# Even layer's input projections as seven products per pair of column blocks, then one phase in which latent and neighbourhood heads take turns unit by unit

## The chip, the cores and the metric

The kernel runs on one core of a Trainium2 chip. The metric is the device time of one execution in microseconds (us). The kernel before was timed three times, 2625.05 to 2626.97 us, with a median of 2626.67 us.

## The reference

One inference step of a two-layer trunk with 640 tokens of width 2048: 512 latent tokens (a grid of 8 rows by 64 columns) and 128 prompt tokens. Every layer is a normalised and modulated mixer with a residual; shift, scale and gate come from `SiLU(cond) @ w_ada`. The even layer comes first and is the one that changes:

```python
h = rmsnorm(x, g_pre) * (1.0 + scale) + shift
# even layer: 4 x 1024 columns for 8 neighbourhood heads, 512 + 256 + 64 + 1024 for 8 latent heads
qa, ka, va, ga, cq, ckv_raw, kpe, gb = _split(h @ w_in, EVEN_SPLITS)
q_mla = (rmsnorm(cq, g_q) @ w_uq).reshape(B, S, MLA_HEADS, MLA_NOPE + MLA_ROPE)
ckv = rmsnorm(ckv_raw, g_kv)
kb, vb = mla_kv(ckv, kpe, w_ukv)
oa = na_latent(qa, ka, va, ctx_k, ctx_v, rpb)      # window of 8 x 16 keys + 128 cached keys, bias rpb
ob = dense_attention(q_mla, [kb_ctx, kb_lat], [vb_ctx, vb_lat], MLA_SCALE)   # 640 keys
y = concatenate([oa * silu(ga), ob * silu(gb)]) @ w_out
x = x + gate * rmsnorm(y, g_post)
```

(Cut and joined from the reference's functions.) Prompt tokens attend to prompt tokens only. The odd layer has one input projection to q, k, v and g, 2048 columns each, and differential attention in 8 heads.

## The kernel before, in words

**Numbers.** Weights and activations are split into a high and a low part: `w_split` (L92) has ScalarE (ACT) cast a 128x1024 tile to `whi` (L82) and VectorE (DVE) subtract for `wlo` (L83). A product takes three passes on TensorE (PE), high by high, high by low and low by high (`passes`, L223). The 640 tokens stand as groups of 384 and 256 columns (`GROUPS`).

**Stages.** In the start stage (L311 to L380) the input is normalised, transposed and modulated, 256 of its 2048 features at a time, and the columns for `cq`, `ckv` and `kpe` are accumulated in seven tiles `cf`. Beside this run the adaptive-scale products `ada` (L175): bursts of eight tiles `araw` of 128x1024 (0.5 MB each, three buffers) loaded on SP's queue. The even mixer follows:

- the *latent preface*: `latent_norm` (L420) squares `cf` on ACT, sums on DVE, reduces over partitions by the matmuls of L429, takes a root on DVE and POOL, broadcasts by L439 and scales (L442), twice; then `w_uq` (matmuls L482) makes the heads' queries, which go to `qm_dram`;
- eight *latent heads* (L495 to L576): keys and values from `w_ukv` (L541), then for each of four 128-row units scores (L558), row maximum on DVE (L273), exponential with row sum on ACT (L274), normalisation on DVE (L564), five transposes, a cast on ACT and a residual on DVE into `pth` and `ptl`, and the value products (L571). Between heads stands `mla_gate`, the gate's projection;
- eight *neighbourhood heads* (L579 to L663): the same with masks added (L641), a window of two or three key tiles and the cached one, and with the head's q, k, g (and, per two heads, v) projections around it.

**Projections.** `proj_T` (L236, matmuls L233) makes one 128-column block for all tokens, 48 matmuls of 384 and 48 of 256 columns; `proj_nat256` (L252, matmuls L249) makes V of two heads in 240 matmuls of 256 columns. Gates pass a tanh on ACT (L267) and a multiply on DVE (L268). `side_step` puts matmuls of `ada` between.

```python
    def proj_T(srcs, emit, groups=(0, 1)):
        ws = [w_split(s) for s in srcs]
        for g in groups:
            n0, n = GROUPS[g]
            emit(proj_group(ws, g, bank("pj")), slice(n0, n0 + n))
        side_step(SIDE)
```

**The odd layer's form.** The output projection `out_proj` (L672) is followed by the odd layer's projections in another form: two 128-column blocks with the input halved give a 2x2 by 2x2 product, made as seven products instead of eight (`PRODUCTS`, `product` with matmuls L830, 24 each of 320 columns). Seven weight tiles and the input halves' sums (`project_pairs`, L848) are made for it on DVE; the results are added up by DVE and ACT from the PSUM banks (`products`, L896). One product of 28 of the pairs needs only the input and is made ahead, in `out_proj` (`early_products`, L836, `NE`). The odd attention (L1037 to L1201) runs in units of scores, transposes, combination and values, which `step` (L1174) advances by one unit at a time.

**Order.** The order on each engine follows from the program's order and from when buffers come free. Nearly all DMAs are on SP's queue and are issued in order.

## Time and profile before

| | us |
|---|---|
| median of three runs | 2626.67 |
| lowest, highest | 2625.05, 2626.97 |
| the profiled execution, its own time | 2620.83 |
| its span in the trace | 2619.1 |
| PE busy in the span | 2532.0 |
| DVE busy | 1534.5 |
| ACT busy | 1116.3 |
| mean granted clock of TensorE (1 is full) | 0.987 |

The sum of a forecast is made against the profiled execution's own time. Busy time is the time in which an engine had an instruction running; listed durations of single matmuls overlap, since they are pipelined, so a pace is a stretch of time divided by the matmuls in it. A row of busy time by windows reads: the window in us from the span's start, its length, then for PE, PEld (TensorE's weight load), DVE, ACT and POOL the busy time and the number of instructions, the share of full clock that TensorE was granted, the share of DMA engines busy, and GB/s. A row of groups reads: line, engine, operation, output and input names, shapes and types, xcount, busy us, mean ns of one, and the engine's idle time just before with what ended it. A row of a timeline reads: start, duration, engine or queue, line, operation; SPq is SP's issuing of DMAs.

### The profile page before, as it was taken

The numbers are of one execution on the slowest core, as the hardware profiler recorded it, in microseconds if no ns is written. First come the engines' busy times: TensorE is split into PE (matmuls) and PEld (weight loads), VectorE is DVE, ScalarE is ACT, GpSimd is POOL, SyncE is SP. The second block draws the span as 40 slices with busy tenths as digits, with TensorE's granted clock in tenths as the row PEclk, the third lists the DMA queues.
The fourth block names the chain that finished last, engine by engine and source line by source line (L and its number), as shares of the span: only waits on it lengthen the run. The fifth ranks groups of instructions, "written<-read, shape, count | busy, mean of one in ns | idle before, by whom it ended". The sixth has DMA issues, their size and how long they took to land. (4 is left out here: it accounts for less than half of the span.)

```text
span 2619.1 us, 42512 instructions
## 1 busy us (share of the span) xinstructions
PE 2532.0 (97%) x16898; PEld 2299.3 (88%) x16898; DVE 1534.5 (59%) x2492; ACT 1116.3 (43%) x2020; POOL 54.0 (2%) x83
## 2 busy tenths in 40 slices
PE   7999999999999999999899999999999989998997
PEld 5779999899989899988789999999999988777876
DVE  5665654534233333443767677777777757874454
ACT  6333333423223222433555344444444447773333
POOL 0000000000000000000000000000000010000000
PEclk9999999999999999999999999999999999998998
DMA  7773322334444443464887344444444457845465
GB/s 292 267 251 117 128 94 103 117 102 140 132 156 158 137 142 133 163 210 140 262 271 266 129 155 160 157 158 151 151 152 150 141 181 273 300 163 189 161 214 196
DMA packets 217111, 455.78 MB, mean 174 GB/s; under 512 B 59664, under 2 KB 104976, under 8 KB 215248
## 3 DMA queue, kind: packets, MB, share of 16 engines
q1 hardware_dynamic: 209648, 436.80, 49.7%
q0 software_dynamic: 3232, 11.67, 1.3%
q10 hardware_dynamic: 4032, 4.59, 0.5%
q8 instruction: 133, 2.18, 0.3%
q14 instruction: 66, 0.54, 0.1%
HBM read 385.54 MB, written 67.44 MB: 173 GB/s over the span
## 5 line engine op out<-in xcount | busy, mean ns | idle before, releaser
L83 DVE TENSOR_TENSOR wlo<-raw,whi 128x1024 fp32r<-128x1024 f32 x458 | 558.2, 1220 | 504.7 <-ACT whi L82 500.5
L82 ACT CAST whi<-raw 128x1024 fp32r<-128x1024 f32 x458 | 479.1, 1046 | 735.7 <-PE pj L724 156.5
L830 PE MATMUL b<-BT,whi 128*128 128x320 f32 x1600 | 355.0, 311 | 4.3 <-ACT whi L82 4.3
L830 PEld LDWEIGHTS b<-BT,whi 128*128 128x128 f32 x1600 | 269.2, 189 | 4.5 <-ACT whi L82 4.5
L830 PE MATMUL b<-BT,wlo 128*128 128x320 f32 x800 | 248.6, 311 | 0.4 <-DVE wlo L83 0.4
L233 PE MATMUL pj<-act0h,whi 128*128 128x384 f32 x512 | 177.9, 348 | 0.0
L233 PE MATMUL pj<-act0h,wlo 128*128 128x384 f32 x512 | 175.1, 342 | 0.0
L233 PE MATMUL pj<-act0l,whi 128*128 128x384 f32 x512 | 173.6, 339 | 0.0
L830 PEld LDWEIGHTS b<-BT,wlo 128*128 128x128 f32 x800 | 151.1, 189 | 0.8 <-DVE wlo L83 0.8
L233 PE MATMUL pj<-act1l,whi 128*128 128x256 f32 x512 | 146.1, 285 | 0.0
L233 PE MATMUL pj<-act1h,whi 128*128 128x256 f32 x512 | 146.0, 285 | 0.0
L233 PE MATMUL pj<-act1h,wlo 128*128 128x256 f32 x512 | 145.6, 284 | 0.0
L184 PE MATMUL ada<-araw,c_s 128*32 128x256 f32 x1536 | 124.5, 389 | 6.5 <-DMA araw<-in_wada 4.1
L830 PE MATMUL b<-B,whi 128*128 128x320 f32 x512 | 113.1, 309 | 0.0
L233 PEld LDWEIGHTS pj<-act0h,whi 128*128 128x128 f32 x512 | 96.8, 189 | 6.6 <-issue 4.1
L830 PE MATMUL pj<-BT,whi 128*128 128x320 f32 x448 | 99.0, 309 | 0.0
L233 PEld LDWEIGHTS pj<-act0l,whi 128*128 128x128 f32 x512 | 96.7, 189 | 2.1 <-issue 1.6
L233 PEld LDWEIGHTS pj<-act1h,wlo 128*128 128x128 f32 x512 | 98.0, 191 | 0.4
L233 PEld LDWEIGHTS pj<-act1l,whi 128*128 128x128 f32 x512 | 98.1, 192 | 0.1
L233 PEld LDWEIGHTS pj<-act1h,whi 128*128 128x128 f32 x512 | 98.0, 191 | 0.1
L233 PEld LDWEIGHTS pj<-act0h,wlo 128*128 128x128 f32 x512 | 96.6, 189 | 1.2 <-issue 1.2
L273 DVE TENSOR_REDUCE smm<-sc 128x1 f32<-128x640 f32 x80 | 65.4, 818 | 43.3 <-PE sc L558 27.0
(491 smaller groups left out, 6309.7 us busy)
## 6 DMA issues: line engine op xcount, KB each, us to landing
araw<-in_wada SPq DMA_DIRECT2D x192, 512.0 KB, 4.5
raw<-in_wout SPq DMA_DIRECT2D x128, 512.0 KB, 4.3
raw<-in_wEna SPq DMA_DIRECT2D x48, 512.0 KB, 3.3
raw<-in_wOq SPq DMA_DIRECT2D x46, 512.0 KB, 4.0
raw<-in_wOk SPq DMA_DIRECT2D x46, 512.0 KB, 3.8
raw<-in_wOg SPq DMA_DIRECT2D x32, 512.0 KB, 3.9
raw<-in_wOv SPq DMA_DIRECT2D x32, 512.0 KB, 3.8
raw<-in_wE SPq DMA_DIRECT2D x16, 512.0 KB, 3.6
```

What stands on the lines that cost most here:

```text
L82: nc.scalar.copy(out=hi, in_=src)
L83: nc.vector.tensor_tensor(out=lo, in0=src, in1=hi.bitcast(F32), op=sub)
L184: mm(ps[32 * kk:32 * kk + 32, x * 256:(x + 1) * 256], lhsT=c_s[:, 4 * q + kk, :], rhs=raw[:, kk * 256:(kk + 1) * 256], start=(q == 0), sto ...
L233: mm(ps[:, :n], lhsT=w[:, c], rhs=a[:, k], start=(k == 0 and x == 0), stop=(k == KT - 1 and x == 2))
L273: nc.vector.tensor_reduce(out=m, in_=src, op=ALU.max, axis=AX.XY if shape3 else AX.X, negate=True)
L830: mm(out, lhsT=w[:, k * 128:(k + 1) * 128], rhs=b[:, k], start=(opens and k == 0 and y == 0), stop=(k == KH - 1 and y == 2), skip_group_ch ...
```

## The change

The even layer's projections take the odd layer's form. `PAIRS` lists for layer 0 four pairs of gate blocks of the latent heads ("m") and, for each neighbourhood head, k with v and q with g: 20 pairs of seven products. `early_products`, `project_pairs` and `products` get the layer as a parameter; `NE` is (20, 28), so every pair of layer 0 has one product made early. The token groups become 320 and 320, and in the start stage `ht`, the modulated input, is also stored to `h_dram`, from where the halves are read back on POOL's queue to make the sums. The seven `cf` tiles are stored to `cf_dram` and read back after the products. All projected blocks go to `pj_dram` (gates with their tanh done, `plain_steps` and `store1`), and each head loads its own.

Behind the products a new PSUM pool is opened (`sc` twice, `tr` and `po` once), the preface runs with `side_step` between its blocks, and then one loop over eight head indices: `start_mla` and `start_na` make the operands of a latent and a neighbourhood head (V of the latter is now transposed on PE), and their units (four and a prompt unit each) alternate in `even_step`: the scores of this unit, the transposes of the last, the values of the one before it, with one or two `ada` steps in turn. The normalisation of a unit moves from DVE to ACT (`normalised`). The output projection takes its weights and heads in the order in which they end (`KORDER0`). The odd layer's work is as before. Core of the diff:

```diff
-GROUPS = ((0, 384), (384, 256))
+GROUPS = ((0, NH), (NH, NH))
-NE, NE1 = 28, 12
+NE = (20, 28)
+NE1 = (4, 8)
...
+    h_dram = [dp.tile([KT, 128, 2, NH], F32, name=f"h_dram{l}") for l in range(2)]
+    cf_dram = [dp.tile([128, NT], F32, name=f"cf_dram{b}") for b in range(7)]
...
+            nc.sync.dma_start(out=h_dram[0][ks].rearrange("k p h n -> p k (h n)"), in_=ht)
...
+        for b in range(7):
+            for x, sl in zip(halves(cf[b]), (slice(0, NL), slice(NL, NT))):
+                nc.sync.dma_start(out=cf_dram[b][:, sl].rearrange("p (h n) -> p h n", h=2), in_=x)
...
+    PAIRS = ([("m", b, "m", b + 1, (i["wE"][b], i["wE"][b + 1])) for b in range(0, 8, 2)]
+             + [(r0, hd, r1, hd, (i["wEna"][hd, x0], i["wEna"][hd, x1])) for hd in range(NA_HEADS)
+                for r0, x0, r1, x1 in (("k", 1, "v", 3), ("q", 0, "g", 2))],
+             [(r0, b, r1, b, (i[w0][b], i[w1][b])) for b in range(2 * DIFF_HEADS)
+              for r0, r1, w0, w1 in (("k", "g", "wOk", "wOg"), ("q", "v", "wOq", "wOv"))])
...
+    def early_products(l, act0):
+        for g in range(NE[l]):
+            out = bank("pj")[:, :NH]
+            product(out, w_split(PAIRS[l][g][4][0][1]), [x[:, KH:] for x in act0], True)
+            xs = xp.tile([128, NH], F32, tag="xs1", bufs=2, name="xs1")
+            nc.scalar.copy(out=xs, in_=out)
+            nc.scalar.dma_start(out=p2_dram[l][g], in_=xs)
+            yield
...
+            def plain_steps(xs, kind, b):
+                if kind == "m":
+                    th = sp.tile([128, 2, NH], F32, tag="th", name="th")
+                    nc.scalar.activation(out=th, in_=xs, func=AF.Tanh, scale=0.5)
+                    nc.vector.scalar_tensor_tensor(out=xs, in0=th, scalar=1.0, in1=xs, op0=ALU.add, op1=ALU.mult)
+                for x, sl in ((xs[:, :, :HL], slice(0, NL)), (xs[:, :, HL:], slice(NL, NT))):
+                    nc.sync.dma_start(out=pj_dram[0][kind][b][:, sl].rearrange("p (h n) -> p h n", h=2), in_=x)
+                if kind == "k":
+                    nc.sync.dma_start(out=o["na_kT"][b].rearrange("p (h n) -> p h n", h=2), in_=xs[:, :, HL:])
+                yield
...
+    xp = space(even, "xs")
+    project_pairs(0, act0, spare, early_products(0, act0))
+    even.close()
+    banks_.close()
...
+    pp = space(banks_, "ps1", True)
+    twice[:] = ["sc"]
...
+    side = (x for l, c in [(0, (16 + n, 17 + n)) for n in range(0, 8, 2)] + [(1, (n, 8 + n)) for n in range(8)]
+            for x in ada(l, c))
...
+    for b in range(7):
+        nc.sync.dma_start(out=cf[b], in_=cf_dram[b])
...
+        for name, src, n in (("kc", i["na_kcT"][hd], 128), ("qf", pj_dram[0]["q"][hd], NT), ("kf", pj_dram[0]["k"][hd], NT),
+                             ("vf", pj_dram[0]["v"][hd], NT), ("vc", i["na_vc"][:, hd * 128:(hd + 1) * 128], 128),
+                             ("sg", pj_dram[0]["g"][hd], NT)):
+            x[name] = np_.tile([128, n], F32, tag=name, bufs=2, name=name)
+            nc.sync.dma_start(out=x[name], in_=src)
+        return x
...
+    def normalised(e, z):
+        nc.vector.reciprocal(out=z, in_=z)
+        nc.scalar.activation(out=e, in_=e, func=AF.Copy, scale=z)
...
+            def scores():
+                ps = half2(bank("sc"))
...
+                        mm(ps[:, h, :NH], lhsT=q, rhs=k[:, h * NH:(h + 1) * NH], start=(n == 0), stop=(n == 4))
+                s["e"] = e = m2.tile([128, NT], F32, tag="e", bufs=3, name="e")
+                z = m2.tile([128, 1], F32, tag="z", bufs=4, name="z")
+                softmax(m2, ps[:, :, :NH], half2(e), z, True)
+                normalised(e, z)
+            def turned():
+                if t % 2 == 0:
+                    H["p"] = [m2.tile([128, 5, 256], F32R, tag=f"pt{n}", name=f"pt{n}") for n in "hl"]
+                pt = bank("tr")
+                transpose_to(pt, s["e"], 5)
+                c = slice((t % 2) * 128, (t % 2 + 1) * 128)
+                hi_lo(pt[:, :NT].rearrange("p (t c) -> p t c", t=5), *[y[:, :, c] for y in H["p"]])
+            def values():
+                if t % 2 == 0:
+                    return
+                if t == 1:
+                    H["po"] = bank("po")
+                po = H["po"]
+                for b in range(5):
+                    for n, (v, pr) in enumerate(passes(vh, vl, *H["p"])):
+                        mm(po[:, (t - 1) * 128:(t + 1) * 128], lhsT=v[:, b, vs], rhs=pr[:, b],
+                           start=(b == 0 and n == 0), stop=(b == 4 and n == 2))
+                if t == 3:
+                    gated(po, x["sg"], slice(0, NL))
+            return scores, turned, values
+        kpf_ = kpf[rows]
...
+    def even_step(u=None):
+        if u is not None:
+            u[0]()
+        if late:
+            late[0][1]()
+        if ends:
+            ends.pop(0)[2]()
+        if late:
+            ends.append(late.pop(0))
+        if u is not None:
+            late.append(u)
+    loads = [(load_mla(0), load_na(0))]
+    n_unit = 0
+    for hd in range(8):
+        xm, xn = loads.pop()
+        for t, units in enumerate(zip(start_mla(hd, xm), start_na(hd, xn))):
+            if t == 1 and hd < 7:
+                loads.append((load_mla(hd + 1), load_na(hd + 1)))
+            for u in units:
+                even_step(u)
+                side_step(1 + n_unit % 2)
+                n_unit += 1
+    even_step()
```

PE at the end of the first norm: `po` and `tr` are the norm's PSUM tiles, `pj` that of a projection, `act0` the input, `BT` an input sum of the seven products, `araw` a tile of `w_ada`. Before:

```order
L233 MATMUL pj<-act0h,whi 128x384
L233 MATMUL pj<-act0l,whi 128x384
L429 MATMUL po<-ones,acc 128x8 x5
L439 MATMUL tr<-dg,ones 128x128 x2
L233 MATMUL pj<-act0h,wlo 128x384
L233 MATMUL pj<-act0h,whi 128x384
L233 MATMUL pj<-act0l,whi 128x384
L439 MATMUL tr<-dg,ones 128x128 x2
```

and with the change:

```order
L352 MATMUL pj<-BT_2244,whi 128x320 x2
L352 MATMUL pj<-BT_2244,wlo 128x320
L191 MATMUL ada<-araw,c_s 32x256 x28
L624 MATMUL po<-ones,acc 128x8 x5
L191 MATMUL ada<-araw,c_s 32x256 x4
L179 MATMUL ada<-ident,ad 128x128 x3
L624 MATMUL po<-ones,acc 128x8 x5
L179 MATMUL ada<-ident,ad 128x128
L634 MATMUL tr<-dg,ones 128x128 x5
L676 MATMUL sc<-cqh,whi 128x384
```

The norm's matmuls stood between matmuls of a gate's projection; now they stand behind the last product, between `ada` steps, and `w_uq` (L676) follows at once.

The norm's operands `cf` are loaded on SP behind the last stores of the products and two more `araw` tiles (seven loads of L583, 128x640 each); before, they were still in SBUF.

SP in the first stage (`araw` tiles of `w_ada`, `wS` the weights of `cf`). Before:

```order
L182 DMA araw<-in_wada 128x1024 x8
L89 DMA raw<-in_wS 128x1024
L89 DMA raw<-in_wS 128x768
L399 DMA gsub<-in_diff_g 128x2
L182 DMA araw<-in_wada 128x1024 x8
```

and with the change:

```order
L189 DMA araw<-in_wada 128x1024
L314 DMA h_dram_138<-ht 128x2x640
L189 DMA araw<-in_wada 128x1024 x7
L95 DMA raw<-in_wS 128x768
L95 DMA raw<-in_wS 128x1024
```

The store of `ht` (L314) is new and stands behind the first tile of a burst, ahead of the other seven.

ACT within two heads (`e` the exponentials, `smm` the row maximum, `z` the row sum, `pth` the cast transposes). Before, in a latent head:

```order
L274 ACTIVATE e,z<-sc,smm 128x640
L82 CAST qh<-raw 128x512
L82 CAST qph<-raw 128x512
L274 ACTIVATE e,z<-tr,smm 128x640
L82 CAST pth<-sc 128x5x128
L82 CAST pth<-tr 128x5x128
L274 ACTIVATE ep,zp<-tr,smm 128x128
L267 ACTIVATE sg<-pj 128x384
L307 COPY ep<-tr 128x128
L82 CAST whi<-raw 128x1024 x2
```

and with the change:

```order
L245 ACTIVATE e,z<-sc,smm 128x640
L88 CAST pth<-tr 128x2x128
L731 ACTIVATE e<-e,z 128x640
L88 CAST pth<-tr 128x128
L876 COPY e<-sc 128x128
L245 ACTIVATE e,z<-e,smm 128x512
L88 CAST pth<-tr 128x5x128
L731 ACTIVATE e<-e,z 128x512
```

The casts of weights and the gates' tanh are gone from here, the normalisation (L731) is new, and a latent unit (640 wide) and a neighbourhood unit (512 or 384) follow each other.

## Rows read from the trace of the kernel before

**Rows 1.** Windows: busy time in the start stage and the even mixer, and the sum.
```profile
0.00:196.30 196.30, 176.07 (x1389) 135.29 (x1390) 117.87 (x280) 84.94 (x153) 3.48 (x12) 1.00 0.77 270
196.30:1098.00 901.70, 894.36 (x6611) 826.06 (x6610) 395.31 (x739) 298.65 (x612) 2.85 (x2) 1.00 0.38 127
...
sum 2619.00, PE 2532.01 PEld 2299.31 DVE 1534.53 ACT 1116.26 POOL 53.97; mean PE 506.40 PEld 459.86 DVE 306.91 ACT 223.25 POOL 10.79
```

**Rows 2.** Windows: matmuls of L249, L233, L830 alone (PE and PEld only).
```profile
842.90:871.80 28.90, 28.90 (x240) 28.80 (x240) 1.00 0.41 137
...
901.20:915.30 14.10, 14.10 (x96) 14.04 (x96) 1.00 0.53 188
...
1339.00:2147.00 808.00, 795.54 (x5376) 792.19 (x5376) 0.99 0.50 165
```

**Rows 3.** Windows: the latent preface, all engines, then L482 alone (PE, PEld).
```profile
196.30:265.00 68.70, 67.38 (x446) 65.11 (x445) 41.21 (x71) 27.02 (x46) 2.85 (x2) 0.98 0.34 119
...
217.70:262.50 44.80, 44.26 (x288) 42.00 (x288) 1.00 0.44 153
```

**Rows 4.** Timeline: the first norm’s matmul and the first cast behind it.
```profile
200.50 1.28 PE L429 MATMUL po<-ones,acc 128*128 128x8 f32 x10
...
211.53 0.73 ACT L82 CAST cqh<-cf 128x640 fp32r<-128x640 f32 x1 [8.97 <-DVE cf L442]
```

**Rows 5.** Groups on ACT: the even mixer; last row: the odd attention.
```profile
L82 ACT CAST whi<-raw 128x1024 fp32r<-128x1024 f32 x91 | 95.4, 1048 | 183.3 <-PE pj L233 98.8 <-PE pj L249 68.4 <-PE pj L541 7.7
L274 ACT ACTIVATE e<-sc,smm 128x640 f32<-128x640 f32 x16 | 12.7, 796 | 44.9 <-DVE smm L273 44.9
...
L82 ACT CAST pth<-tr 128x640 fp32r<-128x640 f32 x16 | 11.1, 696 | 6.9 <-PE tr L172 6.7
...
L267 ACT ACTIVATE sg<-pj 128x384 f32<-128x384 f32 x16 | 7.9, 492 | 10.9 <-PE pj L233 8.9 <-DMA raw<-in_wE 1.3 <-DMA raw<-in_wEna 0.7
...
L267 ACT ACTIVATE sg<-pj 128x256 f32<-128x256 f32 x15 | 5.7, 377 | 0.0
...
L1133 ACT ACTIVATE e<-e,z 128x640 f32<-128x640 f32 x32 | 26.7, 835 | 2.1 <-DVE z L1131 1.8
```

**Rows 6.** Groups on DVE: the even mixer.
```profile
L83 DVE TENSOR_TENSOR wlo<-raw,whi 128x1024 fp32r<-128x1024 f32 x90 | 110.3, 1225 | 204.8 <-ACT whi L82 204.5
L564 DVE TENSOR_SCALAR e<-e,z 128x640 f32<-128x640 f32 x32 | 17.7, 552 | 0.8
...
L273 DVE TENSOR_REDUCE smm<-sc 128x1 f32<-128x640 f32 x16 | 13.2, 824 | 27.0 <-PE sc L558 27.0
...
L83 DVE TENSOR_TENSOR ptl<-tr,pth 128x640 fp32r<-128x640 f32 x16 | 13.2, 824 | 5.1 <-ACT pth L82 5.1
...
L268 DVE SCALAR_TENSOR_TENSOR sg<-sg,pj 128x384 f32<-128x384 f32 x16 | 8.9, 554 | 5.0 <-ACT sg L267 4.9
...
L645 DVE TENSOR_SCALAR e<-e,z 128x512 f32<-128x512 f32 x16 | 7.7, 482 | 0.3
L645 DVE TENSOR_SCALAR e<-e,z 128x384 f32<-128x384 f32 x16 | 6.7, 420 | 0.5
...
L268 DVE SCALAR_TENSOR_TENSOR sg<-sg,pj 128x256 f32<-128x256 f32 x15 | 6.2, 414 | 0.0
```

**Rows 7.** Windows: odd attention, first 24 us, steady part, last 16 us.
```profile
2150.00:2174.00 24.00, 15.70 (x72) 14.67 (x71) 10.03 (x19) 8.90 (x19) 2.51 (x5) 0.67 0.96 345
...
2198.00:2354.00 156.00, 151.91 (x1185) 126.23 (x1184) 128.06 (x315) 118.67 (x309) 12.80 (x15) 1.00 0.71 247
2354.00:2370.00 16.00, 10.58 (x65) 8.74 (x64) 11.31 (x20) 10.88 (x29) 0.00 (x0) 0.89 0.50 158
```

**Rows 8.** Timeline of SP, first stage: two bursts of ada tiles.
```profile
66.00 12.30 SPq L182 DMA_DIRECT2D araw<-in_wada  x8
...
83.54 12.74 SPq L182 DMA_DIRECT2D araw<-in_wada  x8
```

More of the change, by code (lines that the diff above doesn't have):

```diff
@@ L30 @@
 LAM_INIT = 0.8 - 0.6 * math.exp(-0.3 * 1)
+KORDER0 = [b for p in range(4) for b in (8 + 2 * p, 9 + 2 * p, 2 * p, 2 * p + 1)]
 NA_SCALE = 128 ** -0.5
@@ new lines, in model @@
+        nc.sync.dma_start(out=gpost, in_=i["gpost"])
+        accs = cycle("pj", "sc", "po", "pj")
+        for p in range(8):
+            if p == 0:
+                run(first)
+            ws = [w_split(i["wS"][p, :, 0:1024]), w_split(i["wS"][p, :, 1024:1792], 768)]
+            ht = cfp.tile([128, 2, NT], F32, tag="ht", bufs=2, name="ht")
+            for kk in range(2):
+                k = 2 * p + kk
+                for g, (n0, n) in enumerate(GROUPS):
+                    for m, sl in ((0, slice(0, HL)), (1, slice(HL, NH))):
@@ L495, in model @@
[L495 to L503 removed]
+            ks = slice(2 * p, 2 * p + 2)
+            for g, (n0, n) in enumerate(GROUPS):
+                hi_lo(ht[:, :, n0:n0 + n], act[g][0][:, ks], act[g][1][:, ks])
@@ new lines, in model @@
+            nc.sync.dma_start(out=h_dram[0][ks].rearrange("k p h n -> p k (h n)"), in_=ht)
+            if p < 7:
+                run(ada(0, (p + 1, 9 + p), "tr"))
+            for b in range(7):
+                hi, lo = ws[b // 4]
+                for g, (n0, n) in enumerate(GROUPS):
+                    ps = next(accs)
+                    for kk in range(2):
+                        c = ((b % 4) * 2 + kk) * 128
+                        for x, (w, a) in enumerate(passes(hi, lo, *act[g])):
+                            mm(ps[:, :n], lhsT=w[:, c:c + 128], rhs=a[:, 2 * p + kk],
+                               start=(kk == 0 and x == 0), stop=(kk == 1 and x == 2))
+                    dst = cf[b][:, n0:n0 + n]
+                    if p == 0:
+                        nc.scalar.copy(out=dst, in_=ps[:, :n])
+                    else:
+                        nc.vector.tensor_tensor(out=dst, in0=dst, in1=ps[:, :n], op=ALU.add)
@@ new lines, in product @@
+    def product(out, ws, bt, opens):
+        for k in range(KH):
+            for y, (w, b) in enumerate(passes(*ws, *bt)):
+                mm(out, lhsT=w[:, k * 128:(k + 1) * 128], rhs=b[:, k], start=(opens and k == 0 and y == 0),
+                   stop=(k == KH - 1 and y == 2), skip_group_check=True)
+    p2_dram = [[dp.tile([128, NH], F32, name=f"p2_{l}_{g}") for g in range(NE[l])] for l in range(2)]
+    def early_products(l, act0):
[6 more added lines that the diff above has]
+            yield
@@ new lines, in start_mla @@
+        ps = half2(bank("sc"))
+        for h in range(2):
+            for b in range(2):
+                w0 = (e2 * 2 + b) * 128
+                for n, (w, a) in enumerate(passes(hi[:, w0:w0 + 128], lo[:, w0:w0 + 128], ckh, ckl)):
+                    mm(ps[:, h, :384], lhsT=w, rhs=a[:, b, h * 384:(h + 1) * 384], start=(b == 0 and n == 0),
+                       stop=(b == 1 and n == 2))
+        hi_lo(ps[:, :, :384], half2(kh), half2(kl))
+        nc.scalar.copy(out=kf, in_=ps[:, 1, 256:384])
@@ L658, in model @@
-                nc.scalar.copy(out=osb[:, :NL], in_=po)
-                nc.scalar.copy(out=osb[:, NL:], in_=prompt_T_out(np_, [(qf[:, NL:], kf)], vp[:, vs]))
-                sg = np_.tile([128, NT], F32, tag="sg", bufs=2, name="sg")
-                proj_T(i["wEna"][hd, 2], lambda ps, sl: silu2(ps, sg[:, sl]))
-                gate_store(((osb, slice(0, NT)),), sg, 0, hd)
-        run(side)
+                gated(po, sg, slice(0, NL))
+            return scores, turned, values
+        return [unit(b) for b in range(4)] + [prompt_unit(np_, [(qf[:, NL:], kf[:, NL:])], vp, sg, hd)]
@@ new lines, in model @@
+    late, ends = [], []
+    def even_step(u=None):
[20 more added lines that the diff above has]
+                n_unit += 1
```

1031 lines of the change are left out of this document (464 added, 567 removed).

## The prediction

> **What bounds the kernel now.** First read the busy time by stage. In the whole span TensorE (PE) is busy 2532 of 2619 us, and in the even layer's mixer, from 196.3 to 1098.0 us, 894.4 of 901.7; VectorE (DVE) and ScalarE (ACT) are busy 395 and 299 us there [rows 1]. The change lives in that stage, so the question is what PE has to do in it and what else could come to hold it up. I cut the 901.7 us into three parts.
>
> *Projections.* Counts over clean stretches give the true pace of matmuls, without the overlap that their listed durations contain [rows 2]: one 128-column block by `proj_T` (48 matmuls of 384 columns, 48 of 256) takes 14.1 us, a 256-column pair by `proj_nat256` (240 matmuls of 256 columns) 28.9 us. The mixer has 32 of the first and 4 of the second: 451 + 116 = 567 us.
>
> *Latent preface.* From 196.3 to 262.5 us there are the norms and the `w_uq` products, plus one gate projection of 14.1 us: 66.2 - 14.1 = 52 us, of which the `w_uq` matmuls take 44.8 [rows 3].
>
> *The rest.* 902 - 567 - 52 = 283 us, or 35.4 us per head pair (one latent and one neighbourhood head): attention and the adaptive-scale matmuls (`ada`), with the projections interleaved as cover for every softmax wait.
>
> **The change part by part.**
>
> *Seven products instead of eight.* The odd layer runs this form already: 5376 matmuls of 320 columns in 808 us, so 0.1503 us each, all its waits included [rows 2]. The even layer gets 20 pairs of 7 x 24 = 168 matmuls, 3360 in all: 505 us. Against 567 that is **-62 us**. Its weight sums are four DVE operations per pair as in the odd layer, without the rope that the odd layer adds, and the odd layer keeps its pace with DVE as loaded as that. The making of the five operands lies beside the 20 early products, about 71 us of PE work. I put it at nothing more. Bounds: at 0.147 us, the pace inside one projection block (14.1/96), 494 us; with 10 us for operands that come late, 515.
>
> *A preface without cover.* Now the gate projection hides the norm chain. After the change the PSUM pool changes hands, the seven `cf` tiles come back from DRAM, and the order of PE has seven `ada` steps and then the norm's matmuls. SP issues the `cf` loads behind the last stores of the products. From the first norm matmul at 200.50 us to the end of a first cast at 212.26 us the chain took 11.8 us [rows 4]. The loads ahead of it, 2.3 MB of `cf` and three 0.5 MB `ada` tiles, take 14 us at the 270 GB/s of the first stage [rows 1]. Together about 25 us, then the 45 us of `w_uq`: 70 instead of 52, **+18**. Bounds of the gap: 12 us if the loads are hidden, 40 if the second norm and the loads line up behind the first.
>
> *Attention alone.* This is the term that decides. ACT in the stage before is 298.65 us; the change takes 80 of the 91 weight casts away from here (80 x 1.048 = 84) and the tanh (13.6), the preface has about 25 of its own [rows 3, 5], and it adds the normalisation, which moves from DVE: 32 latent units at 0.835 us, the odd layer's price for the same, and 32 smaller ones for which I take 0.6, in proportion to columns (46 us). So ACT comes to 222 us. DVE: 395.3 - 80 x 1.225 (98) - 15 (gates) - 32 (normalisation) - 39 (preface) = 211 [rows 3, 6]. PE, an estimate from the paces of [rows 2] (0.147 us for 320 columns, 0.12 for 256, and 0.12 for what is narrower too): 40 score matmuls of 320 columns, 12 of 384 for keys, 75 of about 256, 39 transposes and some 60 narrow `ada` matmuls per head pair, about 28 us, 222 in all. Three engines, then, each with 26 to 28 us per head pair, and no projection between them. That they overlap fully gives 28 us; no stage does.
>
> The nearest row is the odd layer's attention, which runs the same kind of loop: in its steady part 156 us for six heads, 26.0 each, with DVE busy 21.3 and ACT 19.8 [rows 7]. By DVE, 26.4 x 26.0/21.3 = 32; by ACT, 27.8 x 26.0/19.8 = 36.5. I take 34, and 16 us for filling and draining, as the odd loop's last stretch has it [rows 7]: 8 x 34 + 16 = 288 us. Against 283 that is **+5**, with 3 us for the first head's queries, which make a round trip through DRAM: **+8**. Ends: 238 us (28 per head) and 366 us (the serial chain, below).
>
> *Start.* The activations are also stored to `h_dram`, 5.2 MB, from the queue that loads the `ada` tiles. That is 19 us at 270 GB/s if nothing hides it, nothing if all is hidden. SP issues eight tiles in 12.3 us and the next burst starts at 83.54, so some 5 of 17.5 us are nearly free [rows 8]; but the store stands behind the first tile of a burst and must wait for `ht`, and the other seven are queued behind it. I take **+6**. Groups of 320 and 320 columns cost what 384 and 256 did; the extra small ACT and DVE operations (four for three) lie beside PE, at worst 4 us.
>
> *Handover to the output projection.* The last head's gate projection used to cover it: **+2**, above the drain counted already. All later stages are the same work.
>
> Sum: -62 + 18 + 8 + 6 + 2 = -28 us. The profiled execution took 2620.8 us (span 2619.1 and 1.7 around it), so 2593 by its own clock; it lies 5.8 us below the median of the timed runs, 2626.67, and on that scale the forecast is **2599 us**.
>
> **A rule against it.** In the odd attention's first 24 us PE was busy for 15.7 and its granted clock was 0.67, a mix of the two levels; in the 156 us that followed PE was busy 97% and the clock 1.00 [rows 7]. The Trainium skill, "TensorE: Matmul & The Clock Gate", "Why this matters for your kernels", says that idle gaps between bursts of matmuls put the array back to half its clock. The first of these rows agrees with it, the second shows a loop of this kind that escapes. For the sum I use the second. Were the loop to run at 0.67 throughout, its 27.8 us of PE work would take 41.5 per head, 348 us in all instead of 288.
>
> **The rivals.**
>
> *The units run one after another (slower).* `tr` has one buffer, so a unit's transposes wait until the previous unit's residual has left it, and each softmax passes DVE, ACT, DVE, ACT. Laid end to end, a latent unit costs max 0.824, exponential 0.796, normalisation 0.835, cast 0.696 and residual 0.824 [rows 5, 6], with sums and reciprocals about 4.3 us; the neighbourhood unit about the same with its mask added and two casts. A pair of units is 8.7 us, four pairs and about 9 us for the head's own splits and prompt units 43.7 us: 366 us, 2677. If half the overlap is lost, 39.5 us per head, 332 us and **2643 us**. It decides from 38 us per head on. For it: three engines equally loaded, a chain that crosses between two of them, and no filler but `ada`. Against it: the order on ACT puts another unit's cast or exponential into nearly every wait, and the odd loop reaches 82% of DVE.
>
> *The loop comes near its engines' bound (faster still).* At 30 us per head 256 us, **2567 us**. For it: two independent streams, and 15 `ada` steps to fill PE. Against it: the odd loop does not.
>
> *The clock falls in the loop*, as priced above: **2659 us**.
>
> *The saving is given back by the edges.* A gap of 40 us, 19 in the start, 10 in the operands: 2599 + 15 + 13 + 10 = **2637 us**. That the change does not do what it says would show here too: 3360 matmuls at a pace of 0.165 would save 13 us instead of 62. The same loop in the odd layer speaks against that.
>
> **How the numbers follow.** A measurement of this kernel tells 0.2%, 5 us, from no change. The forecast, 32 to 36.5 us per head with edges as taken, spans 2580 to 2622 and gets 0.56; nearly all of it is faster. The fast rival gets 0.14, the serial one 0.20, the clock 0.03, the edges 0.07. Faster: 0.54 + 0.14 + 0.01 = 0.69. Within 0.2% (2621 to 2632): 0.02 of the forecast, 0.05 of the serial case where it is mildest and 0.03 of the edges, 0.10. Slower: 0.21. The range goes down to 2562, past the fast rival's 2567, and up to 2648, past 2643 and 2637; what lies outside is a loop at its bound below, the fully serial chain and the low clock above, about 0.2. The forecast's own range is 2580 to 2622.
>
> **What would show it.** Right: the products of the even layer at 0.150 us per matmul and 505 us; a PE gap of some 25 us behind them; a head pair every 34 us, with ACT and DVE each busy about 80% of it and PE's clock near 1.00; the first stage ending near 203 us instead of 196. Wrong: a head pair over 38 us with PE waiting for normalised rows and ACT for row maxima means the serial rival; a clock below 0.9 in the loop the clock; `wlo` or `tf` as PE's releaser in the products a DVE that the sums overload; and SP sitting at the `h_dram` store while `ada` waits for its tiles a start that is dearer than 6 us.

## The result, and the profile after

The changed kernel is slower by 0.7%: 2644.9 us, median of four runs (2639.08 to 2647.45), against 2626.04 for the kernel before; the ratio is 1.0069, with a 95% interval of 1.0050 to 1.0087. The forecast was 2599 with 69% for faster; the range, up to 2648, held the time, but the sign was wrong. In what follows a ratio compares with the kernel before as timed in the same session, and a total without a ratio is a single execution, of which it can't be told whether it was a slow one.

The busy time by stage of the changed kernel, cut at its own stage bounds (start, products, the gap to the first `w_uq` matmul, `w_uq`, the loop over head pairs, all that follows), columns as in [rows 1]:

```profile
0.00:208.70 208.70, 180.07 (x1377) 137.19 (x1378) 120.36 (x291) 87.39 (x166) 6.10 (x16) 0.98 0.78 276
208.70:704.00 495.30, 493.52 (x3366) 492.80 (x3368) 340.04 (x369) 208.26 (x291) 3.57 (x5) 1.00 0.48 159
704.00:742.60 38.60, 15.41 (x98) 8.87 (x97) 13.10 (x33) 7.45 (x12) 2.88 (x2) 0.58 0.85 288
742.60:792.40 49.80, 49.77 (x315) 46.37 (x315) 29.76 (x51) 21.46 (x40) 0.00 (x0) 0.95 0.48 148
792.40:1122.40 330.00, 297.28 (x2225) 226.09 (x2221) 204.06 (x481) 203.74 (x476) 0.00 (x0) 0.96 0.64 214
1122.40:2640.90 1518.50, 1460.03 (x8897) 1337.28 (x8897) 1020.85 (x1471) 731.77 (x1253) 47.53 (x69) 0.98 0.57 190
```

Against the stages of before, with the forecast of each term:

| stage | before, us | after, us | difference | forecast |
|---|---|---|---|---|
| start | 196.3 | 208.7 | +12.4 | +6 |
| projections / products | 567 | 495.3 | -71.7 | -62 |
| preface (gap and `w_uq`) | 52 | 88.4 | +36.4 | +18 |
| attention with `ada` | 283 | 330.0 | +47.0 | +8 |
| the rest | 1521.1 | 1518.5 | -2.6 | +2 |

The differences sum to 21.5, that of the two spans is 21.8 (2640.9 - 2619.1). So the products gave more than was forecast, and the start, the preface and the loop took it back. In the loop PE is busy 297 of 330 us, and DVE and ACT 204 each: what the forecast had as three equal engines is one engine well ahead of two.

In the gap, what PE waited for (the waits of PE, 704.0 to 742.6 us; total, times, longest):

```profile
PE ada L191 <- DMA araw<-in_wada: 16.9, 4, 7.9
PE po L624 <- DVE acc L622: 2.9, 2, 2.1
```

And SP's queue at the same time, as a timeline:

```profile
708.68 0.42 SPq L523 DMA_DIRECT2D pj_g<-xs  x1
709.20 0.88 SPq L189 DMA_DIRECT2D araw<-in_wada  x2
710.13 3.73 SPq L583 DMA_DIRECT2D cf<-cf_dram  x7
715.45 0.33 SPq L599 DMA_DIRECT2D lamb<-in_lam  x1
```

The products' last store (L523) is issued at 708.68; only then come the `ada` tiles and `cf`. PE's first norm matmul stands behind `ada` matmuls that wait for these tiles, and they make up the longest wait. They are not what held the norm, though. Its matmuls began when their operand `acc` was ready, 2.09 us after the last of these `ada` matmuls; DVE, ACT and PE in time order:

```profile
721.43 0.23 DVE L658 COPY kpf<-cf 128x128 f32<-128x128 f32 x1 [13.16 <-DMA cf<-cf_dram]
723.08 0.20 ACT L604 ACTIVATE lam<-lam 128x2 f32<-128x2 f32 x1 [15.33 <-DVE lam L603]
723.19 0.72 ACT L618 ACTIVATE acc<-cf 128x640 f32<-128x640 f32 x1
725.53 1.08 PE L191 MATMUL ada<-araw,c_s 128*32 128x256 f32 x8 [1.11 <-DMA araw<-in_wada]
728.71 2.30 PE L624 MATMUL po<-ones,acc 128*128 128x8 f32 x10 [2.09 <-DVE acc L622]
```

The squares that make `acc` (L618 and behind) could start only at 723.19: a copy of a `cf` tile on DVE waited for its load until 721.43, a small exponential for the odd layer (`lam`) stood behind that copy and behind its own load, issued at 715.45 behind `cf`, and the first square stood behind the exponential on ACT. So the late loads held the norm, by way of DVE and ACT.

The steady part of the loop, from the keys of the second head to those of the eighth (six head pairs): first everything, then the `ada` matmuls of L191 alone (PE and PEld), and below them PE's longest waits in it:

```profile
840.60:1076.10 235.50, 222.10 (x1705) 169.08 (x1705) 148.02 (x362) 152.50 (x360) 0.00 (x0) 0.99 0.71 235
...
840.60:1076.10 235.50, 54.34 (x552) 15.06 (x552) 0.99 0.71 235
```

```profile
PE ada L191 <- DMA araw<-in_wada: 5.0, 7, 1.3
PE tr L179 <- DVE ptl L89: 4.1, 6, 1.0
```

A head pair takes 39.25 us, PE is busy for 37.0 of it: 9.1 in the `ada` matmuls and 28.0 in the rest, nearly all of it attention. DVE has 24.7 and ACT 25.4. The loop's 330 us are eight times 39.25 and 16 for filling and draining.

### The profile page after: what moved, and what is told of

The parts are those of the page before. It is cut to its first block, busy times and chain, and to the rows that moved or that the text cites. A ratio compares the mean times of both kernels' runs of the same rounds, so it can differ in the third digit from the quotient of the medians.

```text
span 2640.9 us, 42310 instructions
## 1 busy us (share of the span) xinstructions
PE 2496.1 (95%) x16266; PEld 2248.6 (85%) x16266; DVE 1728.2 (65%) x2695; ACT 1260.1 (48%) x2237; POOL 60.1 (2%) x91
## 5 line engine op out<-in xcount | busy, mean ns | idle before, releaser
L88 ACT CAST whi<-raw 128x1024 fp32r<-128x1024 f32 (+1 forms) x518 | 542.2, 1047 | 853.2 <-PE pj L995 161.5
L89 DVE TENSOR_TENSOR wlo<-raw,whi 128x1024 fp32r<-128x1024 f32 (+1 forms) x518 | 631.3, 1220 | 443.7 <-ACT whi L88 439.1
L352 PE MATMUL b<-BT,whi 128*128 128x320 f32 x2560 | 567.1, 310 | 4.3 <-ACT whi L88 4.3
L352 PEld LDWEIGHTS b<-BT,whi 128*128 128x128 f32 x2560 | 429.9, 189 | 4.5 <-ACT whi L88 4.5
L352 PE MATMUL b<-BT,wlo 128*128 128x320 f32 x1280 | 396.7, 310 | 0.4 <-DVE wlo L89 0.4
L191 PE MATMUL ada<-araw,c_s 128*32 128x256 f32 x1536 | 147.4, 405 | 35.6 <-DMA araw<-in_wada 35.2
L352 PEld LDWEIGHTS b<-B,whi 128*128 128x128 f32 x832 | 139.1, 188 | 0.0
L352 PE MATMUL pj<-act0h,whi 128*128 128x320 f32 x416 | 130.1, 313 | 6.8 <-ACT xs L363 6.8
L352 PE MATMUL pj<-act0h,wlo 128*128 128x320 f32 x416 | 129.4, 312 | 0.0
L352 PE MATMUL pj<-act0l,whi 128*128 128x320 f32 x416 | 129.4, 311 | 0.0
L352 PE MATMUL b<-act0h,whi 128*128 128x320 f32 x416 | 128.5, 309 | 0.0
L191 PEld LDWEIGHTS ada<-araw,c_s 128*32 128x32 f32 x1536 | 40.1, 110 | 83.2 <-DMA araw<-in_wada 47.8
L245 ACT ACTIVATE e<-sc,smm 128x640 f32<-128x640 f32 x96 | 76.6, 798 | 28.6 <-DVE smm L244 27.1
```

What stands on the lines that cost most here:

```text
L88: nc.scalar.copy(out=hi, in_=src)
L89: nc.vector.tensor_tensor(out=lo, in0=src, in1=hi.bitcast(F32), op=sub)
L191: mm(ps[32 * kk:32 * kk + 32, x * 256:(x + 1) * 256], lhsT=c_s[:, 4 * q + kk, :], rhs=raw[:, kk * 256:(kk + 1) * 256], start=(q == 0), sto ...
L245: nc.scalar.activation(out=dst, in_=src, func=AF.Exp, bias=m, accum_out=z)
L352: mm(out, lhsT=w[:, k * 128:(k + 1) * 128], rhs=b[:, k], start=(opens and k == 0 and y == 0), stop=(k == KH - 1 and y == 2), skip_group_ch ...
```

## Experiments

**What sets the loop's pace.** Theory A: PE's own work. Theory S, the serial rival of the prediction: the chain of a unit (maximum, exponential, normalisation, cast, residual). The first run takes all `ada` work out of the loop, and out of the preface.

```diff
-    make_cond()
     side = (x for l, c in ...
...
-                side_step()
     pre_.close()
...
                 even_step(u)
-                side_step(1 + n_unit % 2)
...
     even_step()
+    mctx.close()
+    mctx = ExitStack()
+    mp_ = space(mctx, "mod2")
+    make_cond()
     run(side)
     mctx.close()
```

> All ada steps of the preface and the loop run behind the loop, one after another, with no cover; the loop then holds attention alone. Theory A (the loop stands at PE's own work, some 34 us per head pair of which ada is 8 to 9): the loop, 330 us from its first w_ukv matmul to its last values in the changed kernel, takes 260 to 280 us. Rival S (the softmax chain of the units sets the pace, and ada only fills its waits): it takes 315 us or more. The total is longer in both, since 96 tiles of 0.5 MB have then to be loaded alone, about 170 us.

The loop took 290.1 us (total 2783.49): neither's number. The six steady head pairs (816.5 to 1017.4 us), and PE's longest waits in them:

```profile
816.50:1017.40 200.90, 168.49 (x1114) 151.15 (x1113) 143.73 (x321) 146.16 (x348) 0.00 (x0) 0.97 0.35 103
```

```profile
PE tr L179 <- DVE ptl L89: 11.0, 8, 1.8
PE sc L806 <- ACT e L245: 6.0, 10, 1.4
```

33.5 us per head pair, with PE busy 28.1, DVE 24.0, ACT 24.4. So attention by itself does take longer than any engine's work, and what PE waits for is the units' chain: residuals (`tr` for `ptl`, 11.0 us of that stretch) and exponentials (`sc` for `e`, 6.0). But `ada` is no filler in these waits: 9.1 us of it per head pair lengthen the pair by 5.8.

The second PSUM buffer of the scores goes to the transposes instead, on top of the version whose `ada` tiles come behind the preface (its diff stands with the gap, below):

```diff
-    twice[:] = ["sc"]
+    twice[:] = ["tr"]
```

> As the run without ada in the preface, but in the loop tr has two PSUM buffers and sc one. If the single tr holds the units up (a unit's transposes wait for the residual of the one before, the serial rival's reason), the loop falls from 332 to 315 or less; if the scores need the second buffer more, it rises to 345 or more; within 8 us, neither sets the pace.

The loop rose from 332.4 to 356.5 us (total 2658.71): the scores need the second buffer more than the transposes do. What `tr` would gain from one of its own, beside the two of the scores, this run can't show. The changed loop's waits bound it: PE waits there for residuals in `tr` for 4.1 of 235.5 us, 0.7 per head pair, so the serial rival's reason plays little part with `ada` in the loop.

```diff
-        nc.scalar.activation(out=e, in_=e, func=AF.Copy, scale=z)
+        nc.vector.tensor_scalar(out=e, in0=e, scalar1=z, scalar2=None, op0=ALU.mult)
```

> The units' normalisation goes back to DVE (0.55 us for 640 columns) from ACT (0.83 us); nothing else. Theory A (PE's own work sets the loop's pace): the loop stays within 5 us of 330 and the total within 6 us of 2645. Rival S (the chain of a unit, or ACT, sets it): 64 units with a chain shorter by some 0.25 us each, the loop falls by 10 to 18 us, and the total with it.

The loop fell by 4.4 us to 325.6, the total to 2637.13 (ratio 1.0038, 1.0024 to 1.0052): within A's bound for the loop, somewhat past it for the total. Left to settle it: take PE work away and leave DVE's and ACT's, and take a piece of the chain away and leave PE's work. The third pass of the value products is left out for both kinds of head; the line is shown once.

```diff
-                seq = [(qh[:, qs], kh), (qh[:, qs], kl), (ql[:, qs], kh), (qph[:, qs], kps), (qpl[:, qs], kps)]
+                seq = [(qh[:, qs], kh), (qh[:, qs], kl), (ql[:, qs], kh)]
...
-                    for n, (v, pr) in enumerate(passes(vh, vl, *H["p"])):
+                    for n, (v, pr) in enumerate(passes(vh, vl, *H["p"])[:2]):
```

> The changed kernel with matmuls left out of the loop's units, DVE and ACT doing what they did: two of the five score passes of a latent unit and the third pass of the value products (about 16 + 10 + 5 matmuls per head pair, some 4.5 us of PE, 36 us in all). Theory A (PE's own work sets the loop): it falls from 330 to 300 or less. Rival S (the chain of softmax, cast and residual sets it): it stays above 320.

```diff
     def normalised(e, z):
         nc.vector.reciprocal(out=z, in_=z)
-        nc.scalar.activation(out=e, in_=e, func=AF.Copy, scale=z)
```

> The changed kernel with the units' normalisation left out of the loop (the reciprocal stays): 64 operations of 0.6 to 0.83 us less on ACT, 46 us, and a shorter chain; PE's work is the same. Theory A: the loop stays above 318 (moving it to DVE took 4). Rival S: it falls to 312 or less.

Whole loop and six steady pairs, first with less PE work, then without the normalisation:

```profile
794.90:1099.90 305.00, 265.47 (x1977) 192.13 (x1973) 203.49 (x481) 199.55 (x475) 0.00 (x0) 0.95 0.71 231
838.40:1049.30 210.90, 192.16 (x1462) 140.75 (x1461) 146.62 (x359) 148.04 (x357) 0.00 (x0) 0.99 0.75 244
```

```profile
793.90:1116.70 322.80, 296.80 (x2225) 224.27 (x2221) 203.55 (x481) 162.58 (x412) 0.00 (x0) 0.98 0.67 218
839.50:1071.90 232.40, 223.90 (x1706) 167.70 (x1704) 149.06 (x363) 121.22 (x310) 0.00 (x0) 1.00 0.75 241
```

With 5.0 us less PE work per pair (32.0 busy instead of 37.0) a pair takes 35.15 us, 4.1 less. With 5.2 us less ACT work and a shorter chain it takes 38.7, 0.5 less. The matmuls left out were part of a unit's chain too, so the first run shortens both; the second, and the loop without `ada`, where the chain was left as it was, tell the two apart. So with `ada` in the loop its steady pace is PE's work and a few waits; the chain holds it only below about 34 us. The whole loop took 305.0 and 322.8 us: the second is as A said, the first misses A's "300 or less", since filling and draining gave only 0.4 us of the 25. In the second they gave 4.1 of its 7.2: there the chain does count.

**The gap in front of `w_uq`.** `ada` is kept out of the preface by taking its tiles and its condition vector from a pool that opens behind it:

```diff
-    make_cond()
     side = (x for l, c in ...
...
-                side_step()
     pre_.close()
+    mp_ = space(mctx, "mod2")
+    make_cond()
```

> The 12 ada steps of the preface are taken out of it: their tiles and the condition vector now come from a pool that opens behind the preface, so no ada matmul can stand ahead of the norm, and the steps run in the loop instead. Theory A (PE waits at ada matmuls whose tiles SP can load only behind the last stores of the products, and the norm's matmuls are queued behind them): the gap from the last product to the first w_uq matmul falls from 39 us to 20 to 25, the loop gains at most 5 us, the total falls by 10 to 18 us, to about 2630. Rival R (the gap is the load of cf and the norm's chain, and ada only fills it): the gap stays at 35 to 39 us and the total within 5 us of 2645.

The gap fell from 38.6 to 23.2 us, the number of A; the loop grew by 2.4 and the total is 2637.04 (ratio 1.0043, 1.0024 to 1.0062). A's reason is only half of it. SP and PE in this run:

```profile
692.17 3.21 SPq L582 DMA_DIRECT2D cf<-cf_dram  x7
...
717.09 2.30 PE L623 MATMUL po<-ones,acc 128*128 128x8 f32 x10 [9.27 <-DVE acc L621]
```

With no `araw` tiles ahead of them the `cf` loads go out at 692.17, 15.6 us before the last product ends, instead of 6.1 us after it. From the last product to the first norm matmul it took 24.7 us in the changed kernel and 9.3 here; from there to `w_uq` 13.9 in both. So the 15.4 us are the loads, which the `ada` tiles held up, and not the `ada` matmuls ahead of the norm's on PE. Whether the tiles did it by their place in SP's queue or by the room in SBUF that they took, no run tells.

Of the gain the loop's start lost something to the edit itself. PE waited 12.28 us for its first `ada` matmul:

```profile
786.88 6.70 SPq L681 DMA_DIRECT2D qm_dram<-rr  x2
793.29 0.48 DVE L129 MEMSET c_s<- 128x512 f32 x1
793.64 0.94 SPq L189 DMA_DIRECT2D araw<-in_wada  x2
798.10 1.08 PE L191 MATMUL ada<-araw,c_s 128*32 128x256 f32 x8 [12.28 <-DMA araw<-in_wada]
```

The condition vector `c_s` was now made on DVE behind the rope of the last `w_uq` blocks, ready at 794.0; but what ended the wait was the tile, issued at 793.64 behind the last store of that rope (L681). (A later expectation, below, puts this wait down to the condition vector alone.)

In the next run both norms are made ahead of the products, on top of this:

```diff
+        latent_norm(cf[0:4], 512, gq)
+        latent_norm(cf[4:6], 256, gkv)
         for b in range(7):
             for x, sl in zip(halves(cf[b]), (slice(0, NL), slice(NL, NT))):
...
-        nc.sync.dma_start(out=cf[b], in_=cf_dram[b])
+        nc.gpsimd.dma_start(out=cf[b], in_=cf_dram[b])
```

> On top of the run without ada in the preface: both latent norms run on cf ahead of the products, where the early products can cover them, cf_dram holds the normalised tiles, and they are loaded on POOL's queue. Theory A (the rest of the gap, 23 us, is the loads on SP behind the last stores, 9 us, and the norm's chain, 14): the gap from the last product to the first w_uq matmul falls to 5 to 10 us, products and start stay within 4 us of what they were, the total falls by 13 to 18 us from 2637, to about 2621. Rival R (the chain only moves: PE waits for it in the start stage or at the first products): the products' stretch grows from 495 by 10 us or more, and the total stays at 2632 or above.

The gap fell to 8.2 us, as A said, but the products took 506.3 us instead of 495.1, as R said, and the total is above 2632, as R said too; the two together went from 518.3 to 514.5, and the total is 2634.37 (ratio 1.0036, 1.0023 to 1.0049). Products and gap, then PE's waits from 214 to 300 us:

```profile
213.90:720.20 506.30, 498.37 (x3392) 496.21 (x3391) 348.91 (x401) 209.77 (x292) 12.25 (x17) 1.00 0.50 162
720.20:728.40 8.20, 0.00 (x0) 0.00 (x0) 3.93 (x6) 2.94 (x6) 0.00 (x0) 0.79 0.92 299
```

```profile
PE pj L384 <- ACT xs L395: 3.7, 2, 2.4
PE pj L384 <- DVE wlo L89: 3.5, 3, 1.8
```

The early products that cover the operands' making now cover the norm too. PE waits 7.9 us for ACT and DVE there, 1.8 in the changed kernel: 6 of the 11 us. The others are busy time of PE, 498.4 instead of 493.5 us.

Another way to a short gap: only the `ada` tiles come from the late pool, `cf` is loaded on POOL's queue, and the rope blocks of `w_uq` come first. The last edit was also run alone.

```diff
-        for c in range(6):
+        for c in (4, 5, 0, 1, 2, 3):
             hi, lo = w_split(i["w_uq"][c])
```

> The w_uq blocks that need the rope (the last two of six weight tiles) are made first instead of last; nothing else. Theory A (the first head's operands stand on DVE behind the rope of the last blocks, which itself waits for the stores of the one before): the loop, 330 us in the changed kernel, falls by 6 to 10 us. Rival R (the first head waits for its queries' round trip or for ada tiles): it falls by less than 3.

```diff
-                raw = mp_.tile([128, 1024], F32, tag="araw", bufs=ARAWB, name="araw")
+                raw = (late_ or mp_).tile([128, 1024], F32, tag="araw", bufs=ARAWB, name="araw")
...
-        nc.sync.dma_start(out=cf[b], in_=cf_dram[b])
+        nc.gpsimd.dma_start(out=cf[b], in_=cf_dram[b])
...
-                side_step()
     pre_.close()
+    late_ = space(mctx, "mod2")
```

> Three edits: only the ada tiles come from a pool that opens behind the preface (the condition vector stays early; in the run without ada in the preface the first ada matmul waited 12 us for it), the cf tiles are loaded on POOL's queue, and the rope blocks of w_uq come first. Theory A: the gap from the last product to w_uq falls to 14 to 19 us (the norm's chain and a short load), the loop to 318 to 325, the total to 2618 to 2624, at or a little below the kernel before (ratio 0.997 to 0.999). Rival S (the loop stays at 330 whatever is done at its start): total about 2630.

Theory A missed both times. With the rope first, the loop's first matmul came 6 us earlier, but the loop ended at 1122.5 us, as before the edit (1122.4); the total was 2642.27. In the second the gap was 30.2 us instead of 14 to 19, the loop 340.4, the total 2638.23 (ratio 1.0037, 1.0023 to 1.0052). From the last product to the loop's end it took 411.5 us, against 403.9 with the first edit of this part. What held the norm, in the timeline of this run, whose last product ended at 709.0:

```profile
707.57 0.23 DVE L659 COPY kpf<-cf 128x128 f32<-128x128 f32 x1 [4.98 <-DMA cf<-cf_dram]
...
716.00 0.47 ACT L520 ACTIVATE th<-xs 128x320 f32<-128x320 f32 x1 [4.22 <-DMA pj_g<-xs]
716.37 0.72 ACT L619 ACTIVATE acc<-cf 128x640 f32<-128x640 f32 x1
...
721.89 2.30 PE L625 MATMUL po<-ones,acc 128*128 128x8 f32 x10 [12.88 <-DVE acc L623]
```

On POOL's queue the `cf` loads were issued at 692.96, no earlier than on SP's in the first edit of this part (692.17), and landed later: the copy of `cf` (L659) ran 1.4 us before the last product's end, there 6.3. It stood on DVE ahead of the products' last sums and waited 5 us; then the first square of the norm (L619) stood on ACT behind the last gate's tanh, which waited 4.2 us for its buffer's store. An operand gains nothing by an early load while the operation on it is queued behind others.

**The start.** The store of `ht` on POOL's queue (shown), on ACT's (the same line with `nc.scalar`), and with seven of its eight stores left out:

```diff
-            nc.sync.dma_start(out=h_dram[0][ks].rearrange("k p h n -> p k (h n)"), in_=ht)
+            nc.gpsimd.dma_start(out=h_dram[0][ks].rearrange("k p h n -> p k (h n)"), in_=ht)
```

> The store of ht goes to POOL's queue instead of SP's; nothing else moves. Theory A (SP waits at the store for ht, and seven ada tiles are queued behind it): the first stage, 208.7 us in the changed kernel and 196.3 before, ends at about 199, the total falls by 8 to 11 us. Rival R (the 5.2 MB more of traffic cost bandwidth, whichever queue they are on): it ends at 205 or later, the total falls by less than 4 us.

> The store of ht on ACT's queue. Leaving seven of eight stores out ended the first stage at 202.9 instead of 208.7. If it is SP's in-order issue that makes the store dear (POOL's queue being slower for other reasons), the stage ends at 203 to 205; if it is the traffic, at 207 or later.

> Of the eight stores of ht seven are left out, and the sums of the seven products read the first one's two rows eight times over (the same bytes read, wrong operands); nothing else changes. The first stage ends at 207 to 213 us in the runs so far, 196.3 in the kernel before. Theory A (the 5.2 MB stored beside the ada tiles are what lengthened it, whichever queue they are on): it ends at 195 to 200. Rival R (the groups of 320 and 320, their one operation more per step on ACT and DVE, or the late first tile): it ends at 205 or later.

The first stage ended at 211.1 us with POOL's queue (2653.43 us in all, ratio 1.0091, 1.0068 to 1.0114), at 209.7 with ACT's (2651.4), and at 202.9 without the stores (2637.21); in the ten runs in which nothing in this stage was changed it ended at 207.4 to 214.0. So for this stage the queue doesn't matter and the traffic does, 5 to 11 us of it by the one run without the stores. The Trainium skill, "DMA: Bandwidth & Descriptors", section "Issuing engines are not separate DMA queues", says the same of the queues: DMAs started by different engines share the same 16 DMA engines, and a second issuing engine saves only the issuing. The 6.6 us that are left between 202.9 and 196.3 need another cause, and as single executions that differ by up to 6.6 us without an edit they are no firm number. PE's waits in this stage, of the changed kernel from 50 us on, then of the kernel before from 45 us on:

```profile
PE ada L191 <- DMA araw<-in_wada: 4.8, 8, 1.4
PE pj L324 <- ACT act0h L88: 3.6, 4, 2.7
PE sc L324 <- ACT act0h L88: 1.6, 2, 0.9
PE po L324 <- DVE act0l L89: 1.0, 2, 0.7
PE sc L324 <- DVE act0l L89: 1.0, 2, 0.5
PE pj L324 <- DVE act0l L89: 0.8, 2, 0.4
```

```profile
PE pj L374 <- DVE act0l L83: 1.4, 2, 0.8
PE pj L374 <- ACT act0h L82: 0.9, 2, 0.6
```

It waits 8 us for the split of the modulated input, where the kernel before waited 2.3: four scalings per 128 rows for three, and the split behind them. In the run without the stores PE is idle 4.5 us longer than in the kernel before and busy 2.1 longer, at a granted clock of 0.98 instead of 1.00. That the scalings make up the idle part was read from the traces and not tried by itself.

**Versions.** First the norms ahead and the normalisation on DVE; then the late `ada` tiles, the rope first and the normalisation on DVE; then all of it.

> The run before and the units' normalisation on DVE, both together. If the two act on different stretches their gains add: loop 4 to 6 us shorter than in the run before, total about 2616, 0.3 to 0.4% below the kernel before. If not, it stays within 2 us of the run before.

> The run before with the normalisation on DVE, which took 4 us off the loop by itself: loop 314 to 321, total 2614 to 2620, ratio 0.995 to 0.998. If ACT was not what held the units up in the shorter loop, within 2 us of the run before.

> All that helped, together: norms ahead of the products, ada tiles behind the preface, condition vector early, rope blocks first, normalisation on DVE. Gap plus products were 514 us with the norms ahead and 525 to 527 without, the loop from the end of w_uq 318 with the normalisation on DVE: total 2631.5 less 8 to 10, about 2622, at or just below the kernel before (ratio 0.997 to 1.000). If gains of the stages don't add, 2628 or more.

They took 2631.78 (ratio 1.0025, 1.0015 to 1.0036), 2631.54 (1.0012, 1.0001 to 1.0023) and **2617.94 us (0.9967, 0.9956 to 0.9978)**. The first two missed their 2616 and 2614 to 2620: the gains did not add, and the loop of the second took 328.2 us instead of 314 to 321. The last one came out 4 us below its 2622 and beats both kernels, the one before by 0.3%. Its stages, cut as above (the loop's first matmuls now overlap the end of `w_uq`):

```profile
209.90:718.20 508.30, 501.15 (x3392) 499.23 (x3391) 350.33 (x405) 209.93 (x294) 12.24 (x17) 0.99 0.50 162
718.20:728.90 10.70, 0.04 (x1) 0.00 (x0) 3.40 (x6) 2.90 (x6) 0.00 (x0) 0.61 0.76 233
728.90:771.40 42.50, 39.22 (x240) 37.30 (x241) 31.47 (x45) 15.88 (x30) 0.00 (x0) 0.94 0.64 181
771.40:1097.00 325.60, 311.21 (x2355) 234.12 (x2355) 223.23 (x540) 169.42 (x421) 0.00 (x0) 0.99 0.74 240
```

From the last product to the loop's end it takes 378.8 us, against 418.4 in the changed kernel; the products take 13 more.

## Why the prediction was wrong

*Attention alone: the step that failed.* It put PE at "about 28 us, 222 in all" per head pair, `ada` included, and from that drew "Three engines, then, each with 26 to 28 us per head pair". Measured: 37.0 on PE, 24.7 on DVE, 25.4 on ACT. The sum had some 21 us for attention and 7.2 for 60 `ada` matmuls; it is 28.0 and 9.1, for 92. The count of attention's matmuls was not far off, 166 for the 186 of the run without `ada`, but the price was, 0.13 us each for 0.15; likely because the paces were taken from long runs of one kind of matmul [rows 2], while the loop changes kind every few. The price from the odd loop, 34 us by DVE's and ACT's load, is near what the loop takes without `ada`, 33.5, but partly by luck: by the loads that were measured, 24.7 and 25.4, the same scaling gives 30 and 33. The 16 us of filling and draining are right too. So the step that failed is the size of PE's work: PE set the pace, not DVE and ACT. With 37 us of PE work, at the 94% that PE reaches here, the term is 330 instead of 288.

The rows of before said so. The "rest" of 283 us was got by taking projections and preface from a stage in which PE was busy 99% [rows 1], so nearly all of it was PE work: 35.4 us per pair, 6.8 of them in the `ada` matmuls (54.2 us in that mixer) and 28.6 in the rest, near the 28.0 that the loop has. A forecast of 34 per pair had PE do less than its own work.

*Products.* -71.7 for -62: 3360 matmuls in 495.3 us are 0.1474 each, the lower bound that was given, not the odd layer's 0.1503 [rows 2].

*Preface.* +36.4 for +18. The gap is 38.6 us for "about 25", near the upper bound given, 40, but not by a second norm lined up behind the first. Cut at the lines shown above: 5.2 us until SP issues the first tile behind the last store, 12.2 until the last `cf` load has landed (the loads were priced at 14), 7.3 for the copy, the exponential and the squares up to the first norm matmul, and 13.9 from there to `w_uq` (priced at 11.8, from the first norm matmul to a first cast [rows 4]). So the loads and the chain were about right; SP's wait and the squares ahead of the first norm matmul were left out. The Trainium skill, "TensorE: Matmul & The Clock Gate", section "The mechanism", says that matmuls start and end in program order. The trace agrees, the ten matmuls of the norm began behind the waiting `ada` matmuls; but they began 2.09 us behind the last of them, with their operand, so the order on PE cost the norm nothing here. The other 5 us are `w_uq`, 49.8 for 45: its first 7.4 us ran at a granted clock of 0.63, the rest at 1.00 (1.00 throughout in [rows 3]).

*Start.* +12.4 for +6. The store cost what was taken or a little more, 5 to 11 us; the small operations, put beside PE "at worst 4 us", are the likely rest, which is not shown.

*Handover.* -2.6 for +2: nothing is lost there.

*The rivals.* "The units run one after another" gave 2643 with 39.5 us per head, and the time was 2644.9 with 39.25; but its mechanism was not what happened. Its sign, a pair over 38 us "with PE waiting for normalised rows", came only in its first half: PE waits 13.4 of the 235.5 us, for all causes together, and a shorter chain hardly moved the steady pace. That agreement is chance. (The chain does set the pace once `ada` is gone, at 33.5.) The clock's rival did not come: 0.99 in the steady loop, though 0.85 in the 48.2 us in which it fills. The clock fell furthest where PE was busy least, to 0.58 in the gap, with 15.4 of 38.6 us busy. The edges' rival was partly right: the gap came near its 40 us, the start, +12.4, stayed under its 19, and the products gave 10 us more instead of costing 10; its loop, 34 us per head, is not what was measured.

## What to carry to other kernels

When a stage in which one engine is busy 99% is split into a part with that engine's bulk work and a part without it, count that engine's work in the second part first: it is the remainder of its busy time, and no overlap of the others gets below it. Work that filled waits in the old order is not free in the new one. And an in-order queue is read for what stands ahead of the first instruction that matters: three of the gaps here (`cf` loads behind stores and `ada` tiles on SP, a copy ahead of sums on DVE, a tanh ahead of squares on ACT) were of that kind. The longest wait in a list need not be the one that counts: PE's 16.9 us for `ada` tiles ended before the norm's operand was there.

## What was not expected of the hardware

The same `ada` matmuls cost more in the loop: 692 of them take 69.4 us of PE's busy time, 100 ns each, where 750 took 54.2 us in the mixer of before, 72 ns each; before, then after (PE and PEld):

```profile
196.30:1098.00 901.70, 54.18 (x750) 19.81 (x750) 1.00 0.38 127
792.40:1122.40 330.00, 69.44 (x692) 18.75 (x688) 0.96 0.64 214
```

That would be up to 19 us of the loop's 47. They now run in shorter bursts between matmuls of another kind. Two bursts, each with the matmul behind it; the first is the loop's, the second of the kernel before:

```profile
930.06 0.62 PE L191 MATMUL ada<-araw,c_s 128*32 128x256 f32 x2
930.61 0.33 PE L179 MATMUL tr<-ident,ep 128*128 128x128 f32 x1
...
282.05 1.49 PE L184 MATMUL ada<-araw,c_s 128*32 128x256 f32 x22
283.47 0.41 PE L558 MATMUL sc<-kh,qh 128*128 128x320 f32 x1
```

From its first start to the next matmul's, a burst of two takes 0.55 us and one of 22 takes 1.42. In the six steady pairs 552 matmuls stand in 76 bursts, 27 of them of six or fewer; in the mixer of before 750 stand in 54, five of them so short. Bursts of eight take a median 0.57 us in both kernels, so the traces put the difference down to the length of the bursts; no run changed it alone.

Four runs of the changed kernel lie within 8.4 us and four of the kernel before within 1.9; but in a later session 23 runs of the kernel before spread over 13.4 us (2620.56 to 2634.00), so this is no difference between the two. In the profiled executions the end of the first stage alone moves by 6.6 us between kernels that do not differ there (207.4 to 214.0).
